# Sums, weight split, stores and turns moved in a streaming encoder layer in float32

## The chip, the cores and the metric

One core of one Trainium2 chip runs the whole step. The metric is the device time of one execution in microseconds (us). Five engines matter: TensorE (PE), whose weight loads (PEld) overlap its multiplications; VectorE (DVE); ScalarE (ACT); GpSimd (POOL); and SyncE (SP), which issues most of the DMAs. ACT issues DMAs as well.

## The reference

A layer works on two inputs: 512 new frames of a prompt, and 64 new frames of a running stream (the sample) with 512 cached frames. The model has 2048 channels.

```python
hn = rmsnorm(x, g_norm1)
proj = hn @ w_in
q, k, v, gb, gc, hc = jnp.split(proj, [...], axis=-1)
q = rmsnorm(q.reshape(B, T, N_HEADS, HEAD_DIM), g_q)      # 8 heads of 128
k = rmsnorm(k.reshape(B, T, N_HEADS, HEAD_DIM), g_k)
...
o_attn = stick_breaking_blocks(q, k_all, v_all, P)        # strictly causal, no softmax
u = gc * hc
o_conv = gb * (conv_w[0] * u[t-2] + conv_w[1] * u[t-1] + conv_w[2] * u[t])
mix = jnp.concatenate([rmsnorm(o_attn, g_attn_out), rmsnorm(o_conv, g_conv_out)], axis=-1)
x = x + mix @ w_out
h2 = rmsnorm(x, g_norm2)
x = x + (jax.nn.silu(h2 @ w_gate) * (h2 @ w_up)) @ w_down  # 5632 hidden channels
```

The outputs are the frames of both inputs, their new keys and values, and the convolution's state.

## The kernel before

The 512 + 64 frames are handled as one block of 576 columns, in two halves of 288. Each operand of a product is split in two rounded parts (hi and lo), and PE multiplies three times: hi with hi, lo with hi, hi with lo. The large products (part of the input projection, the output projection, gate, up and down) are done in blocks by a scheme with seven products instead of eight; the products of a unit are numbered `p_` from 1 to 7, and the units are worked off in a fixed list.

PE's order is the order of the program. Beside it runs a pipeline of generators: `product` and `multiply` call `pipe.tick()` after every step of three multiplications, and a generator that yields n goes on n ticks later. So a number in a `yield` or in `spawn` places a step among PE's multiplications. DVE, ACT, POOL and SP follow the program where `manual_schedule` names them (the start, and everything from the last gate and up units on); elsewhere a scheduler puts their instructions in order by its own estimates.

**The start.** Seven loads bring the prompt's frames (`load_x`), three the sample's (`load_s`), and the first weight comes in quarters (`load_w0`), the first of them on ACT's queue. PE turns frames by multiplying with the identity (`turn_samples`, `turn_x`), ACT copies them out of PSUM, and DVE scales and splits them (lines 374 and 375).

**The first head.** `head(0)` takes up the q product begun at the start and goes on with k and v. `norm_evac` turns a product into 32x32 blocks, squares and sums it; `rest`, `lag` ticks later, lets PE add the sums up over the partitions (L654), forms 1/sqrt (L658 to L663), scales and turns the rows back (L664, L668), scales by channel (L669) and splits (L230, L231). `attend` computes the scores (L723). `third_weight` splits the fourth weight tile (whi, wlo: L177, L178); the third was split in `head(0)`.

**The end.** The down product has 37 units for eight blocks of 256 output channels. `run` adds the products into `acc` tiles (L1592 copies a product out of PSUM, L1612 adds on DVE, L1614 on POOL), and after the last unit of a block `store_y` writes it out. `turn_blocks` turns 32x32 blocks on DVE (L1781) and stores pieces of 32 channels (L1770): four stores for the prompt's frames and four for the sample's. `work`, used for the very last unit, turns on PE (L1789, L1792), copies back on ACT (L1794, L1798) and stores whole rows of 128 channels (L1750, L1752, L1800). Some blocks are "lone" (each half in a tile of its own), others are pairs of halves in one tile. Weights of the down product are loaded into `raw_a` and `raw_b` (L1468), as soon as DVE has used up what was in them.

Of the kernel before, what the change touches and what calls it, by code (L numbers as in the profile page):

```python
# [16 lines left out]
P = 128  # L17
TP = 512
# [76 lines left out]
def tile_hybrid_stream_step(  # L95
# [100 lines left out]
    def third_weight():  # L196
        split_weight(nc.vector)
        yield from ()

    def next_weight():  # L200
        i = pos[0]
        pos[0] += 1
        end = first_out if i < first_out else first_block
        while len(raws) < min(i + 2, end):
            load_weight()
        if i == 2:
            pipe.spawn(third_weight(), 14)
        while len(ready) < min(i + 2, end) and i != 2:
            split_weight(nc.vector)
        while len(raws) < min(i + 3, end):  # L210
            load_weight()
        out = ready[i]
        ready[i] = None
        return out

    pipe = Pipeline()
# [76 lines left out]
    gqs = const.tile([P, 1], F32, name="gqs")  # L293
# [14 lines left out]
    def col(name, i=0):  # L308
        return vec[:, rows[name] + i : rows[name] + i + 1]
# [26 lines left out]
    xin, xsn = {}, {}  # L336
# [6 lines left out]
    def load_s(c):  # L343
        k0, k1 = SCH[c]
        xsn[c] = hpool.tile([TS, (k1 - k0) * P], F32, name=f"xsn{c}")
        nc.sync.dma_start(out=xsn[c], in_=xs[:, k0 * P : k1 * P])

    def turn_samples(c):
        k0, k1 = SCH[c]
# [42 lines left out]
    with tc.manual_schedule(engines={mybir.EngineType.Activation, mybir.EngineType.DVE, mybir.EngineType.SP}):  # L392
# [5 lines left out]
        def load_w0(q):  # L398
            (nc.sync if q else nc.scalar).dma_start(out=raw3[:, 4 * q : 4 * q + 4, :], in_=src[:, 4 * q : 4 * q + 4, :])

        load_w0(0)
        load_x(0)
        load_s(0)
        nc.sync.dma_start(out=g1raw, in_=g_norm1[0].rearrange("(r c) -> r c", c=P))
        load_x(1)
        load_x(2)
# [295 lines left out]
    kw = dict(start=False, skip_group_check=True)  # L702

    def attend(h, st):
        yield 15 + (13 if h == 0 else 0)
        qf, qh, ql, kf, kh, kl, kcT, cV = (st[n] for n in ("qf", "qh", "ql", "kf", "kh", "kl", "kcT", "cV"))

        z = [ps_z.tile([P, 512], F32, tag=f"z{i}", name=f"z{i}") for i in range(3)]
# [45 lines left out]
        kb = st["kb"]  # L754
# [97 lines left out]
    def head(h):  # L852
        st = {}
        st["cK"] = t1.tile([P, TP], F32, tag="cK", name="cK")
        st["cV"] = t1.tile([P, 4, P], F32, tag="cV", name="cV", bufs=2)
        for q in range(4):
            nc.sync.dma_start(out=st["cK"][32 * q : 32 * (q + 1), :].rearrange("t (b c) -> t b c", c=32),
                              in_=ck[:, h, 32 * q : 32 * (q + 1)].rearrange("(b t) c -> t b c", t=32))
        nc.sync.dma_start(out=st["cV"], in_=cv[:, h, :].rearrange("(i p) d -> p i d", p=P))
        for n in ("q", "k"):  # L860
            st[n + "f"] = t1.tile([P, T], F32, tag=n + "f", name=n + "f")
            st[n + "h"] = t1.tile([P, TP], F32R, tag=n + "h", name=n + "h")
            st[n + "l"] = t1.tile([P, TP], F32R, tag=n + "l", name=n + "l")
        st["kb"] = t1.tile([P, T], F32, tag="kb", name="kb")
        q_evac = norm_evac("q", gqs, st["qf"], st["qh"], st["ql"], 13 if h else 25)
        k_evac = norm_evac("k", col("gk"), st["kf"], st["kh"], st["kl"], 16 if h else 6, st["kb"], attend(h, st))
        pipe.spawn(keys_cached(st, 20 if h else 52))
        if h == 0:
            for ps, (a, b) in zip(q0ps, HALVES):
                q_evac(ps, a, b)  # L870
            row_diagonals()
            split_weight(nc.vector)
            pipe.spawn(row_eps(), 23)
            pipe.spawn(row_scale(), 29)
            project(k_evac, (None, "z1"))
        else:
            project(q_evac)
            project(k_evac)
        Ev = t1.tile([P, T], F32, tag="E", name="Ev", bufs=2)

        def v_evac(ps, a, b):
            nc.vector.tensor_tensor(out=Ev[:, a:b], in0=ps, in1=R1[:, a:b], op=ALU.mult)

        project(v_evac, ("z2", None) if h == 0 else (None, None))
        pipe.spawn(values(h, st, Ev))
# [341 lines left out]
    for k_, (n, p_) in enumerate(corder):  # L1227
# [7 lines left out]
        if n == NCU - 1 and p_ in (6, 7, 4):  # L1235
            q = {6: 1, 7: 2, 4: 3}[p_]
# [503 lines left out]
    def store_y(n, c, i):  # L1740
# [22 lines left out]
        def blocks(f, ap):  # L1763

            n = ap.shape[1]
            n_p = max(min(TP - f, n), 0)
            for y, t0, t1, g, eng in ((yp, 0, n_p, f, nc.sync), (ys, n_p, n, f + n_p - TP, nc.scalar)):
                for q in range(4 if t1 > t0 else 0):
                    b0 = cs.start + 32 * q
                    eng.dma_start(out=y[g : g + t1 - t0, b0 : b0 + 32].rearrange("(b t) c -> t b c", t=32),  # L1770
                                  in_=ap[32 * q : 32 * (q + 1), t0:t1].rearrange("t (b c) -> t b c", c=32))

        def turn_blocks():
            if (d, c) in both:
# [8 lines left out]
            blocks(f, all_)  # L1783

        def work():
            yield 4
            po = misc("pot")[:, : 3 * P]
            for q in range(2):
                nc.tensor.transpose(po[:, q * P : (q + 1) * P], src[:, k0 + q * P : k0 + (q + 1) * P], ident)  # L1789
# [12 lines left out]
                put(f0 + k0, ob[:, 0, :])  # L1802
                put(f0 + k0 + P, ob[:, 1, :])
            if rest:
                put(rest[1], obs[:nr], nc.scalar)

        pipe.spawn(work() if n == NU - 1 else turn_blocks())

# [104 lines left out]
```

## Time and profile before

| | |
|---|---|
| median of three runs | 2362.01 us (2360.82 to 2364.43) |
| the profiled execution | 2360.45 us, span 2358.7 us |
| PE busy | 2335.9 us, 99% |
| DVE busy | 1894.6 us, 80% |
| ACT busy | 1134.9 us, 48% |
| POOL busy | 300.3 us, 13% |
| granted clock of PE | 0.999 of full speed |

The profile is of one execution. Its timeline gives for each instruction the start and the duration in us, the engine, the line of the kernel, what is written and read, and in brackets how long the engine was idle before it and what ended that. An engine with a q behind its name (SPq, ACTq) is that engine's sequencer, which issues DMAs. The table of waits adds up such idle times: us in total, times, longest.

### The profile page before, as it was taken

To read this page: it belongs to the slowest core of one execution; us is meant where nothing else is said; L and a number is where in the kernel's file an instruction comes from. 1 tells how busy PE (TensorE), PEld (TensorE's weight loads), DVE (VectorE), ACT (ScalarE), POOL (GpSimd) and SP (SyncE) were. 2 spreads that over 40 slices of the span, in tenths; PEclk is the share of its full clock that TensorE was granted. 3 is DMA by queue.
4 is the path that set the end of the run, shared out by engine and by line. 5 is a ranking of instruction groups with operands and counts; after the bars stand their busy time and mean duration, and the time that the engine had idled before them with its cause. 6 is when DMAs were issued, how large, how long until landed. Compare 5 with 4: busy or idle time off the path is not lost.

```text
span 2358.7 us, 43730 instructions
## 1 busy us (share of the span) xinstructions
PE 2335.9 (99%) x17551; PEld 2325.3 (99%) x17551; DVE 1894.6 (80%) x2828; ACT 1134.9 (48%) x1975; POOL 300.3 (13%) x401
## 2 busy tenths in 40 slices
PE   8999999999999999999999999999999999999998
PEld 8999999999999999999999999999999999999998
DVE  8666666788887899888888888888888777987896
ACT  6655555444445555444444444444444444444443
POOL 1111111422121220000000000000000002431222
PEclk9999999999999999999999999999999999999999
DMA  8565563773468555344344444444444936885554
GB/s 268 153 172 142 139 166 104 240 242 114 124 236 227 173 174 160 122 154 151 122 153 141 134 153 142 133 153 132 144 153 132 359 115 206 223 236 199 190 145 87
DMA packets 588996, 395.75 MB, mean 168 GB/s; under 512 B 100222, under 2 KB 577912, under 8 KB 588792
## 3 DMA queue, kind: packets, MB, share of 16 engines
q1 hardware_dynamic: 574968, 375.95, 51.2%
q0 software_dynamic: 8624, 16.22, 3.3%
q8 instruction: 137, 2.24, 0.4%
q10 hardware_dynamic: 5200, 0.79, 0.2%
q14 instruction: 67, 0.55, 0.1%
HBM read 301.46 MB, written 91.44 MB: 167 GB/s over the span
## 4 chain that ended last, share of the span: by engine, by line
PE 89%; DVE 5%; DMA 3%; issue 1%; ACT 1%; SPq 0%; POOL 0%; ACTq 0%; POOLq 0%; DVEq 0%
PE psy L1582 34%; PE psw L1582 17%; PE pj L221 13%; PE psx L1582 8%; PE psy L1086 6%; PE pjo L221 4%; PE psw L1086 3%; PE psx L1086 1%; DMA raw_a<-in_w_out_dram 1%; DVE whl L231 1%; PE po L794 1%; PE z L723 1%; DVE whl L1058 1%; DMA out_dram<-acc 0%; DVE x L375 0%
## 5 line engine op out<-in xcount | busy, mean ns | idle before, releaser
L1582 PE MATMUL psy<-h_s,whl 128*128 128x288 f32 x2787 | 413.5, 295 | 1.1 <-ACT part L1592 1.1
L221 PE MATMUL pj<-x,whi 128*128 128x288 f32 x1856 | 388.6, 298 | 0.2
L1582 PEld LDWEIGHTS psy<-h_s,whl 128*128 128x128 f32 x2787 | 384.8, 189 | 1.8 <-ACT part L1592 1.8
L231 DVE TENSOR_TENSOR whl<-raw_a,whl 128x1024 fp32r<-128x1024 f32 (+4 forms) x296 | 318.2, 1076 | 54.6 <-ACT whl L230 53.1
L1582 PE MATMUL psw<-t,whl 128*128 128x288 f32 x2400 | 347.0, 294 | 0.0
L1582 PEld LDWEIGHTS psw<-t,whl 128*128 128x128 f32 x2400 | 327.8, 188 | 0.0
L230 ACT CAST whl<-raw_a 128x1024 fp32r<-128x1024 f32 (+4 forms) x296 | 267.5, 906 | 113.1 <-issue 35.4
L221 PEld LDWEIGHTS pj<-x,whi 128*128 128x128 f32 x1856 | 303.6, 189 | 1.4 <-DVE x L375 0.7
L221 PE MATMUL pj<-x,wlo 128*128 128x288 f32 x928 | 274.3, 296 | 0.1
L231 DVE TENSOR_TENSOR whl<-raw_b,whl 128x1024 fp32r<-128x1024 f32 (+5 forms) x190 | 200.2, 1054 | 69.5 <-ACT whl L230 68.2
L230 ACT CAST whl<-raw_b 128x1024 fp32r<-128x1024 f32 (+5 forms) x190 | 164.9, 871 | 170.3 <-issue 73.5
L1592 ACT COPY part<-psy 128x288 f32<-128x288 f32 x242 | 96.4, 398 | 284.9 <-PE psy L1582 262.0
L1582 PE MATMUL psy<-t2t,whl 128*128 128x288 f32 x1212 | 183.0, 294 | 0.8 <-ACT part L1592 0.8
L1582 PE MATMUL psy<-b22m,whl 128*128 128x288 f32 x1212 | 183.3, 295 | 0.1
L221 PEld LDWEIGHTS pj<-x,wlo 128*128 128x128 f32 x928 | 174.7, 188 | 0.7 <-DVE wlo L442 0.3
L1582 PE MATMUL psx<-h_s,whl 128*128 128x288 f32 x1185 | 173.6, 294 | 0.0
L1582 PEld LDWEIGHTS psy<-t2t,whl 128*128 128x128 f32 x1212 | 167.8, 188 | 1.1 <-ACT part L1592 1.1
L1582 PEld LDWEIGHTS psy<-b22m,whl 128*128 128x128 f32 x1212 | 168.2, 188 | 0.4 <-ACT part L1592 0.4
L1582 PEld LDWEIGHTS psx<-h_s,whl 128*128 128x128 f32 x1185 | 162.4, 188 | 0.0
L1361 POOL DMA_DIRECT2D hid_dram<-form x3 | 2.2, 749 | 947.6 <-DVE form L231 947.6
L230 ACT CAST whl<-s 128x1024 fp32r<-128x1024 f32 (+5 forms) x81 | 72.2, 892 | 102.8 <-PE psw L1582 99.4
L1582 PE MATMUL psy<-t,whl 128*128 128x288 f32 x576 | 106.5, 294 | 0.0
(474 smaller groups left out, 4297.4 us busy)
## 6 DMA issues: line engine op xcount, KB each, us to landing
hid_dram<-form SPq DMA_DIRECT2D x147, 288.0 KB, 2.3
raw_a<-in_w_in_dram SPq DMA_DIRECT2D x41, 1024.0 KB, 5.8
raw_a<-in_w_gate_dram SPq DMA_DIRECT2D x22, 1024.0 KB, 5.7
raw_a<-in_w_up_dram SPq DMA_DIRECT2D x22, 1024.0 KB, 5.8
raw_b<-in_w_gate_dram SPq DMA_DIRECT2D x22, 1024.0 KB, 6.5
raw_b<-in_w_up_dram SPq DMA_DIRECT2D x22, 1024.0 KB, 6.6
h_s<-hid_dram SPq DMA_DIRECT2D x10, 2016.0 KB, 12.8
raw_a<-in_w_out_dram SPq DMA_DIRECT2D x16, 1024.0 KB, 6.4
```

Source lines behind the costliest of these rows:

```text
L221: mm(ps, w_[:, k, csl], x_, start=(k == 0 and n == 0), stop=(k == nk - 1 and n == 2))
L230: nc.scalar.copy(out=hi, in_=src)
L231: (lo_eng or nc.vector).tensor_tensor(out=lo, in0=src, in1=hi.bitcast(F32), op=ALU.subtract)
L723: mm(zb[i], a_[:, kk], b_[:, q0:TP], start=(n == 0), stop=False, skip_group_check=True)
L794: mm(po[:, i * P : 512], a_[:, i, :], b_[:, : 512 - i * P], stop=(i == 0 and n == 2), **kw)
L1058: tt(out=whl[:, 1], in0=src, in1=whl[:, 0].bitcast(F32), op=ALU.subtract)
L1086: mm(ps, whl[:, w_, j, :], x_, start=(start and j == 0 and q == 0), stop=(j == m - 1 and q == 2), skip_group_check=True)
L1361: q.dma_start(out=hid_dram[fp][2 * n - 2 : 2 * n].rearrange("f p t -> p f t"), in_=t.bitcast(F32))
L1582: mm(ps, whl[:, w_, j, :], x_, start=(start and j == 0 and q == 0), stop=(j == len(xs_) - 1 and q == 2), skip_group_check=True)
L1592: nc.scalar.copy(out=t, in_=st["y"])
```

## The change

It does four things. In the first head, five numbers of ticks move. At the start, the sample's first frames are loaded by ACT's queue ahead of the first weight quarter, which then follows the prompt's first frames in the program. At the end, SP issues the sample's stores that ACT issued in `turn_blocks`. And `work`, with its turns on PE, is used for the last units of three blocks instead of one; for the two added ones it begins after nine ticks and gives its rest to SP.

```diff
-            pipe.spawn(third_weight(), 14)
+            pipe.spawn(third_weight(), 19)
...
-        nc.sync.dma_start(out=xsn[c], in_=xs[:, k0 * P : k1 * P])
+        (nc.sync if c else nc.scalar).dma_start(out=xsn[c], in_=xs[:, k0 * P : k1 * P])
...
-        load_w0(0)
         load_x(0)
         load_s(0)
+        load_w0(0)
...
-        yield 15 + (13 if h == 0 else 0)
+        yield 15 + (4 if h == 0 else 0)
...
-        q_evac = norm_evac("q", gqs, st["qf"], st["qh"], st["ql"], 13 if h else 25)
-        k_evac = norm_evac("k", col("gk"), st["kf"], st["kh"], st["kl"], 16 if h else 6, st["kb"], attend(h, st))
+        q_evac = norm_evac("q", gqs, st["qf"], st["qh"], st["ql"], 13 if h else 31)
+        k_evac = norm_evac("k", col("gk"), st["kf"], st["kh"], st["kl"], 16 if h else 15, st["kb"], attend(h, st))
...
-            for y, t0, t1, g, eng in ((yp, 0, n_p, f, nc.sync), (ys, n_p, n, f + n_p - TP, nc.scalar)):
+            for y, t0, t1, g in ((yp, 0, n_p, f), (ys, n_p, n, f + n_p - TP)):
                 for q in range(4 if t1 > t0 else 0):
...
-                    eng.dma_start(out=y[g : g + t1 - t0, b0 : b0 + 32].rearrange("(b t) c -> t b c", t=32),
+                    nc.sync.dma_start(out=y[g : g + t1 - t0, b0 : b0 + 32].rearrange("(b t) c -> t b c", t=32),
...
         def work():
-            yield 4
+            quick = n == NU - 1
+            yield 4 if quick else 9
...
-                put(rest[1], obs[:nr], nc.scalar)
-
-        pipe.spawn(work() if n == NU - 1 else turn_blocks())
+                put(rest[1], obs[:nr], nc.scalar if quick else nc.sync)
+
+        pipe.spawn(work() if n in sorted(last)[-3:] else turn_blocks())
```

DVE in the first head, before, from the end of the q chain to the end of the k chain (ql is the split of q, wlo the low part of the fourth weight, sums, ms, t, r, Ek and kf the steps of k):

```order
L231 TENSOR_TENSOR ql<-qf,qh 128x512
L178 TENSOR_TENSOR wlo_812<-raw_a,whi_811 128x1024
L678 TENSOR_REDUCE sums<-sq 128x9
L178 TENSOR_TENSOR wlo_812<-raw_a,whi_811 128x1024
L658 TENSOR_SCALAR ms<-ss,rpad_t 128x18
L850 STREAM_TRANSPOSE kcT<-cK 128x512
L661 TENSOR_SCALAR t<-y 128x18
L662 TENSOR_TENSOR t<-t,ms 128x18
L663 TENSOR_SCALAR r<-t,y 128x18
L664 TENSOR_TENSOR Ek<-Ek,r 128x576
L668 STREAM_TRANSPOSE kf<-Ek 128x576
```

The same place after the change (the first ms, t, t and r are now those of q):

```order
L658 TENSOR_SCALAR ms<-ss,rpad_t 128x18
L178 TENSOR_TENSOR wlo_829<-raw_a,whi_828 128x1024
L661 TENSOR_SCALAR t<-y 128x18
L678 TENSOR_REDUCE sums<-sq 128x9
L662 TENSOR_TENSOR t<-t,ms 128x18
L178 TENSOR_TENSOR wlo_829<-raw_a,whi_828 128x1024
L663 TENSOR_SCALAR r<-t,y 128x18
L664 TENSOR_TENSOR Eq<-Eq,r 128x576
L668 STREAM_TRANSPOSE qf<-Eq 128x576
L850 STREAM_TRANSPOSE kcT<-cK 128x512
L658 TENSOR_SCALAR ms<-ss,rpad_t 128x18
L231 TENSOR_TENSOR ql<-qf,qh 128x512
```

The fourth weight moved from behind the q chain to inside it, ahead of the q rows' scaling and turning, and the k chain from behind the weight to behind both.

SP at the end, before, around the blocks of acc_t2z and acc_m1z (one pair) and the next (raw_a and raw_b are the down weights):

```order
L1468 DMA raw_b<-in_w_down_dram 128x10x256
L1770 DMA out_dram<-acc_t2z 32x16x32 x4
L1770 DMA out_dram<-acc_m1z 32x16x32 x4
L1468 DMA raw_a<-in_w_down_dram 128x10x256
L1770 DMA out_dram<-acc_z 32x16x32 x4
L1770 DMA out_dram<-acc_ax 32x16x32 x4
```

The same place after the change:

```order
L1468 DMA raw_b<-in_w_down_dram 128x10x256
L1770 DMA out_dram<-acc_t2z 32x16x32 x4
L1770 DMA out_dram<-acc_t2z 32x2x32 x4
L1770 DMA out_dram<-acc_m1z 32x16x32 x4
L1770 DMA out_dram<-acc_m1z 32x2x32 x4
L1468 DMA raw_a<-in_w_down_dram 128x10x256
L1770 DMA out_dram<-acc_z 32x16x32 x4
L1770 DMA out_dram<-acc_z 32x2x32 x4
```

The four small stores of each block, which stood on ACT, now stand on SP behind the four large ones, and the weight load behind all sixteen.

PE in the first of the two units that turn on PE now, in the product that follows the unit's second (before, only multiplications stand here; the line numbers of `work` are one higher after the change):

```order
L1582 MATMUL psw<-h_s_9012,whl 128x288 x3
L1582 MATMUL psw<-b22m_10290,whl 128x288 x3
L1790 MATMUL pot<-ident,acc_21412 128x128 x2
L1793 MATMUL pot<-ident,acc_21412 32x128
L1582 MATMUL psw<-t_6_10169,whl 128x288 x3
L1582 MATMUL psw<-h_s_9011,whl 128x288 x3
```

Two full turns and one of the last 32 frames stand among the multiplications of a running product.

More of the change, by code (lines that the diff above doesn't have):

```diff
@@ L1766, in blocks @@
             n_p = max(min(TP - f, n), 0)
-            for y, t0, t1, g, eng in ((yp, 0, n_p, f, nc.sync), (ys, n_p, n, f + n_p - TP, nc.scalar)):
+            for y, t0, t1, g in ((yp, 0, n_p, f), (ys, n_p, n, f + n_p - TP)):
                 for q in range(4 if t1 > t0 else 0):
                     b0 = cs.start + 32 * q
-                    eng.dma_start(out=y[g : g + t1 - t0, b0 : b0 + 32].rearrange("(b t) c -> t b c", t=32),
-                                  in_=ap[32 * q : 32 * (q + 1), t0:t1].rearrange("t (b c) -> t b c", c=32))
+                    nc.sync.dma_start(out=y[g : g + t1 - t0, b0 : b0 + 32].rearrange("(b t) c -> t b c", t=32),
+                                      in_=ap[32 * q : 32 * (q + 1), t0:t1].rearrange("t (b c) -> t b c", c=32))
         def turn_blocks():
```

## Prediction

> **What bounds the kernel now.** I read the page first, then the table of waits for PE, then the timeline of each engine where a wait stands, and the chain of work that ended last.
>
> ```profile
> span 2358.7 us, 43730 instructions
> PE 2335.9 (99%) x17551; PEld 2325.3 (99%) x17551; DVE 1894.6 (80%) x2828; ACT 1134.9 (48%) x1975; POOL 300.3 (13%) x401
> ```
>
> PE is without work for 2358.7 - 2335.9 = 22.8 us. The change takes away no multiplication, so 22.8 us is all that it could win. Where PE waits, the table of waits says (us in total, times, longest):
>
> ```profile
> PE psx_s L352 <- DMA xsn<-in_x_sample_dram: 5.4, 1, 5.4
> PE ss L654 <- DVE sums L678: 2.5, 2, 1.7
> PE psy L1582 <- ACT part L1592: 1.9, 3, 0.8
> PE psw L1582 <- DVE acc L1612: 0.6, 1, 0.6
> PE pot L1789 <- POOL acc L1614: 0.2, 1, 0.2
> ```
>
> These five are the waits that the edits can reach: the start, the sums of the first head, and the last 50 us. Together they are 10.6 us. From 100 us to 2240 us the edits leave PE's order as it is, and I cost that stretch at nothing: DVE and ACT swap a few steps in the second and third head, where PE waits for neither.
>
> **The start.** The sample's first frames now go out on ACT's queue, ahead of the first weight quarter, instead of behind the prompt's frames on SP's.
>
> ```profile
> 1.32 3.94 DMA xsn<-in_x_sample_dram
> 5.40 0.66 PE psx_s L352 x4
> 8.09 0.53 DVE x L374
> 26.68 0.83 DVE x L375
> ```
>
> This is the chain: the load, the turns on PE, then DVE making frames back to back until 27.5 us, so what PE wins at 5.4 us reaches DVE and the rest. But PE's turn also waits for the identity and its neighbours on POOL:
>
> ```profile
> 2.39 2.45 POOL L268 TENSOR_SCALAR_AFFINE_SELECT acA<-acA 128x128 f32<-128x128 f32 x7
> ```
>
> POOL ends at 4.84. So the turn moves from 5.40 to 4.9 at best, 0.5 us. The load is issued at about 0.84 instead of 1.32, which is 0.5 us too. The first weight quarter leaves 0.5 us later; its cast stands behind two copies on ACT, at 7.9 us, and I see no wait there now. If that cover were gone, the start would lose up to 0.5 us. I take 0.35 us won, between -0.5 and +0.5, nearer the gain because the bytes on the way are the same and only their order changes.
>
> **The first head.** Five numbers move: the sums of q are multiplied (L654) at tick 31 instead of 25, those of k at 15 instead of 6, the fourth weight is split at 19 instead of 14, and attention begins 4 + 15 ticks after the sums of k instead of 13 + 15. 15 + 19 = 34 = 6 + 28, so PE meets the scores (L723) after the same multiplications as now.
>
> ```profile
> 43.11 0.40 PE L654 MATMUL ss<-sums,acA 128*128 128x18 f32 x2 [0.80 <-DVE sums L678]
> 51.96 0.37 PE L654 MATMUL ss<-sums,acA 128*128 128x18 f32 x2 [1.72 <-DVE sums L678]
> 63.39 0.28 PE L723 MATMUL z<-qh,kh 128*128 128x256 f32 x1
> 49.13 1.05 ACT L177 CAST whi<-raw_a 128x1024 fp32r<-128x1024 f32 x1 [0.40 <-DMA raw_a<-in_w_in_dram]
> 50.22 1.23 DVE L178 TENSOR_TENSOR wlo<-raw_a,whi 128x1024 fp32r<-128x1024 f32 x1 [0.76 <-ACT whi L177]
> 51.36 0.45 DVE L678 TENSOR_REDUCE sums<-sq 128x9 f32<-128x288 f32 x1
> 52.86 0.17 DVE L658 SCALAR_TENSOR_TENSOR ms<-ss,rpad_t 128x18 f32<-128x18 f32 x1
> ```
>
> The two waits are 0.80 and 1.72 us, 2.52 in all. The sums of q are ready at 43.1, and PE got to them at 42.3 and will now come six ticks later (a tick is three multiplications, 0.40 us) with the diagonals (1.3 us) in between, at about 46: that wait goes. Those of k hang on the fourth weight: ACT stands at the weight's load until 49.13, and DVE does a half of the weight (50.22) ahead of the sums (51.36). The new order on DVE keeps that half ahead of the sums. They end at about 52.0. PE got there at 51.96 - 1.72 = 50.24; 0.80 earlier and nine ticks later is 53.0. That wait goes too, with 1 us to spare.
>
> What is late next are the scores. In the new order both halves of the fourth weight stand ahead of the rest of the q chain, and the k chain comes behind that. The durations:
>
> ```profile
> 46.49 0.78 DVE L668 STREAM_TRANSPOSE qf<-Eq 128x576 f32<-128x576 f32 x1
> 48.12 0.62 ACT L230 CAST qh<-qf 128x512 fp32r<-128x512 f32 x1
> 55.81 0.78 ACT L669 ACTIVATE kf<-kf,vec 128x576 f32<-128x576 f32 x1 [2.28 <-DVE kf L668]
> 57.16 0.56 DVE L231 TENSOR_TENSOR kl<-kf,kh 128x384 fp32r<-128x384 f32 x1 [0.65 <-ACT kh L230]
> ```
>
> From 50.22: two halves, the sums and the small steps between, 3.0 us, to 53.2; the q rows scaled and turned, 0.15 + 0.8 + 0.78, to 54.9; on ACT the scaling (0.78, as for k) and qh (0.62), a little overlapped, to 56.3; the k chain's two ACT steps 0.5, to 56.8; its small DVE steps and one half of the values between them 1.1, to 57.9; scaled and turned 1.55, to 59.45; scaled on ACT and cast 1.35, to 60.8; kl 0.55, to 61.35. PE, 2.52 us earlier, arrives at 63.39 - 2.52 = 60.87. So about 0.5 us comes back as a wait at L723, and 2.0 us are left. The load of the weight bounds this from both sides: landing as early as PE gains at the start, 2.5 us are left; 2 us later, none. The cached keys and weight of the second head are issued some 2 us later, since DVE's turn of the first head's cached keys is; they have 10 us before ACT asks for them.
>
> **The end.** Now the sample's stores are issued by ACT, and ACT stands at them:
>
> ```profile
> 2313.80 4.71 ACTq L1770 DMA_DIRECT2D out_dram<-acc  x8
> 2318.55 0.40 ACT L1592 COPY part<-psy 128x288 f32<-128x288 f32 x1 [4.47 <-DMA out_dram<-acc]
> 2342.84 2.01 ACTq L1770 DMA_DIRECT2D out_dram<-acc  x4
> 2319.01 0.67 PE L1582 MATMUL psy<-t2t,whl 128*128 128x288 f32 x3 [0.82 <-ACT part L1592]
> 2345.40 0.67 PE L1582 MATMUL psy<-h_s,whl 128*128 128x288 f32 x3 [0.79 <-ACT part L1592]
> 2347.87 0.67 PE L1582 MATMUL psw<-h_s,whl 128*128 128x288 f32 x3 [0.58 <-DVE acc L1612]
> ```
>
> A copy that frees PE's bank (L1592) waits behind eight stores for 4.47 us, and PE waits 0.82 us for the copy; the same again at 2345 (0.79), and DVE, held by the late cast behind it, costs 0.58. With the stores on SP, ACT has none of these, and the POOL wait of 0.2 hangs on the same late copies: 2.19 + 0.2 = 2.4 us go. DVE also loses six turns there.
>
> Against this stand TensorE's turns for two more units: four lone blocks of three turns, and a pair of pairs with 2 + 2 + 3 + 3, 22 in all. The chain of work prices three:
>
> ```profile
> 2352.44 0.22 PE pot L1789 x2
> 2352.66 0.12 PE pot L1792
> ```
>
> 22 x 0.113 = 2.5 us, all on PE. The turned rows are added at least nine ticks (3.6 us) before PE asks; the adds of now end within 2 to 3 us, so I charge no wait.
>
> [...]
>
> SP now issues 16 stores for a finished pair where it issued 8, and the next weight load of the down product stands behind them.
>
> ```profile
> 2271.43 1.96 SPq L1770 DMA_DIRECT2D out_dram<-acc_t2z  x4
> 2257.55 5.21 SPq L1770 DMA_DIRECT2D out_dram<-acc_z  x8
> 2264.49 0.40 SPq L1468 DMA_DIRECT2D raw_b<-in_w_down_dram  x1
> 2271.92 0.73 ACT L230 CAST whl<-raw_b 128x640 fp32r<-128x640 f32 x1 [2.10 <-DMA raw_b<-in_w_down_dram]
> 2272.68 0.82 DVE L231 TENSOR_TENSOR whl<-raw_b,whl 128x640 fp32r<-128x640 f32 x1 [0.97 <-ACT whl L230]
> 2274.95 5.94 PE psy L1582 x45
> ```
>
> Four stores take 1.96 us, 0.49 each. Sixteen from 2257.55 end at 2265.4, so the load slips from 2264.49 by 1 us. ACT already waits 2.10 us for it, and DVE ends that operand at 2273.5. PE's 45 multiplications from 2274.95 are three products; the second, at 2274.95 + 1.98 = 2276.93, is the first to use it. The slack is 3.4 us, so a slip of 1 us is hidden four times over. The copies behind that cast on ACT are not late, since the 1.95 us of stores there are gone.
>
> Last, the tail behind PE's last work. SP's last stores wait for ACT's (waits of SP in the last 13 us):
>
> ```profile
> SPq L1752 <- DMA out_dram<-raw_b: 1.5, 2, 1.0
> SPq L1750 <- DMA out_dram<-raw_b: 0.4, 1, 0.4
> ```
>
> With the slow 32-row stores gone from the last 15 us and another order of the semaphores, I expect part of these 1.9 us back, 0.6 (between 0 and 1).
>
> The end: -2.4 + 2.5 - 0.6 = -0.5 us. It would be +2.5 if no wait went, -1.5 if all of them and the whole tail did.
>
> **The sum.** -0.35 - 2.0 - 0.5 = -2.85 us. The profiled execution took 2360.45 (1.75 outside its span), so 2357.6 for one like it. The median of the runs is 2362.01, 1.56 above it; against that I predict 2359.2. That is 0.12%; about 0.2% (4.7 us) is what a measurement of this kernel tells from no change.
>
> **The rivals.** (1) *The loads fall behind the stores on SP: slower.* If an issue in a row of 16 costs more than 0.65 us, the load slips by over 3.4 us and PE waits. The eight issues at 2257.55 took 5.21 us, a gap included, 0.65 each. At 0.8 us the load leaves at 2270.35, 5.9 us late, PE waits 2.4 us for it, at four such loads: 9.6 us, 2368.8. Against it: 0.49 for four in a row, with ACT issuing at the same time.
>
> (2) *The scores take the place of the sums.* If the fourth weight lands 2 us later, or DVE's new order runs worse than I added up, PE waits 2.5 us at L723 in place of 2.5 at L654: 2361.2. For it: my sum already has 0.5 us of it.
>
> (3) *A turn costs PE its whole record.*
>
> ```profile
> L1789 PE MATMUL pot<-ident,acc 128*128 128x128 f32 x8 | 1.7, 290 | 0.6 <-DVE acc L1612 0.3 <-POOL acc L1614 0.2
> ```
>
> At 290 ns, 22 turns are 6.4 us instead of 2.5: 2363.1. Against it: the chain has two in 0.22 us, since they are pipelined. [...]
>
> (4) *More goes than I count.* All of the start (0.5), all of the sums (2.5), the whole tail and DVE's relief (1.5 to 2): about -4.8, 2357.2, at the edge of what can be told.
>
> **How the numbers follow.** Forecast 0.64; rival 1 0.08; rival 2 0.13; rival 3 0.05; rival 4 0.10. Only rival 1 is slower by over 0.2%: 0.08. Rival 4 and a little of the forecast are faster by over 0.2%: 0.12. Within: 0.80. The range runs from rival 4 less 1.4 us of scatter (the three runs spread 3.6 us) to rival 3: 2355.8 to 2363.1; rival 1 is left out.
>
> **What would show it.** Right: no wait of PE at L654 in the first head, a wait of under 1 us at L723 near 61 us; the first turn near 4.9 us; no wait of PE for L1592 after 2240 us; 22 more turns 0.11 us apart; down loads issued about 1 us later relative to the stores, with no wait of PE. Wrong: a wait of PE for whl after 2260 us (rival 1), 2 us at L723 (rival 2), turns spaced 0.27 us (rival 3).

## The result, and the profile after

The changed kernel takes 2357.62 us (median of 18 runs, 2355.32 to 2360.17), the kernel before 2361.86 (18 runs on the same chip, 2359.14 to 2364.43): a ratio of 0.9983, 95% interval 0.9977 to 0.9989. That is 4.0 us less. The gain is less than the 0.2% that the prediction took for the least that a measurement tells, but a ratio of 1 lies outside the interval. The forecast was 2359.2, the range 2355.8 to 2363.1. The profiled execution took 2357.63 us, 2.82 less than that of before; the sum had said 2.85. Of all runs below, one of the kernel with the sample's stores on SP alone took 3250.84 us at a granted clock of 0.655, and its ratio leaves that run out.

The head of the page after, and four rows of PE's table of waits (us in total, times, longest):

```profile
span 2355.9 us, 43774 instructions
PE 2335.7 (99%) x17573; PEld 2326.5 (99%) x17573; DVE 1890.2 (80%) x2822; ACT 1138.5 (48%) x1989; POOL 298.6 (13%) x401
```

```profile
PE psx_s L352 <- POOL acA L268: 4.9, 1, 4.9
PE psy L1086 <- DVE whl L1058: 2.8, 3, 1.0
PE ss L500 <- ACT sq L230: 1.7, 1, 1.7
PE z L723 <- DVE kl L231: 0.2, 1, 0.2
```

The rows for L654 are gone, and the first turn waits 0.5 us less, as forecast. The second row was 1.8 us before: a wait has grown in the middle, where I had charged nothing.

**The first head** went as worked out. PE's timeline after, then DVE's:

```profile
45.74 0.29 PE L654 MATMUL ss<-sums,acA 128*128 128x18 f32 x2
52.34 0.29 PE L654 MATMUL ss<-sums,acA 128*128 128x18 f32 x2
60.78 0.39 PE L723 MATMUL z<-qh,kl 128*128 128x256 f32 x1 [0.21 <-DVE kl L231]
```

```profile
50.87 0.44 DVE L678 TENSOR_REDUCE sums<-sq 128x9 f32<-128x288 f32 x1
60.16 0.56 DVE L231 TENSOR_TENSOR kl<-kf,kh 128x384 fp32r<-128x384 f32 x1 [1.39 <-ACT kh L230]
```

Both sums are met without a wait, those of k 1.0 us after they are ready. kl ends at 60.7; the forecast was 61.35, and the cast of the fourth weight started 0.58 us earlier than before (48.55 for 49.13). PE waits 0.21 us for kl (forecast 0.5). By the starts of the first three scores the wait costs 0.57 us: they are at 63.39, 63.51 and 63.63 before, at 60.19, 60.78 and 61.00 after. So at the third score PE leads by 2.63 us, of which 0.5 to 0.8 is the start's.

**The middle** gives most of that lead back. First before, then after: ACT's cast for a form of the attention (hf, one of the blocks and differences of blocks that the seven products take), and PE's products in the convolution (L1086).

```profile
476.38 0.43 ACT L230 CAST hf<-o_ob 128x288 fp32r<-128x288 f32 x1 [3.75 <-DMA form_dram<-hf]
489.46 3.41 PE L1086 MATMUL psx<-x,whl 128*128 128x288 f32 x24 [1.45 <-DVE cv L1110]
```

```profile
475.34 0.43 ACT L230 CAST hf<-o_ob 128x288 fp32r<-128x288 f32 x1 [4.99 <-DMA form_dram<-hf]
482.38 0.40 PE L1086 MATMUL psy<-x,whl 128*128 128x288 f32 x1 [0.47 <-ACT whl L1055]
483.64 3.31 PE L1086 MATMUL psy<-x,whl 128*128 128x288 f32 x23 [0.86 <-DVE whl L1058]
488.43 3.44 PE L1086 MATMUL psx<-x,whl 128*128 128x288 f32 x24 [1.48 <-DVE cv L1110]
...
733.86 5.03 PE L1086 MATMUL psy<-forms,whl 128*128 128x288 f32 x36 [0.56 <-ACT part L1095]
745.94 5.06 PE L1086 MATMUL psy<-forms,whl 128*128 128x288 f32 x36 [0.70 <-ACT part L1095]
```

ACT wants a buffer whose store has not landed. It stood 3.75 us for it before and 4.99 after (and 0.31 at a store just ahead), so of the 2.6 us by which ACT came earlier 1.0 is left, and the casts behind it make PE wait twice. PE leaves the place 1.03 us ahead. At 734 and 746 us ACT stands at weights still on their way (3.13 and 3.28 us; 2.81 and 2.82 before), PE waits 0.56 and 0.70 us (0.23 and 0.25 before), and at 751 us its lead is 0.09. This second loss need not be a price of the lead: between 660 and 752 us PE loses 0.2 to 1.1 us against the profile of before in each of the other profiles, the end alone, which lags, 0.5.

**A stretch at half clock.** The windows of before, then of after, behind the sums of the second norm (columns: window, its length, busy time of the five engines with instructions, granted clock, DMA share, GB/s):

```profile
884.00:886.00 2.00, 2.00 (x11) 2.00 (x12) 2.00 (x4) 0.89 (x2) 0.00 (x0) 0.67 0.99 321
886.00:888.00 2.00, 2.00 (x10) 2.00 (x9) 2.00 (x3) 1.05 (x1) 0.00 (x0) 0.50 1.09 392
888.00:890.00 2.00, 2.00 (x16) 2.00 (x16) 2.00 (x4) 0.93 (x1) 0.00 (x0) 0.97 0.75 271
```

```profile
884.00:886.00 2.00, 1.86 (x14) 1.86 (x15) 2.00 (x5) 0.89 (x2) 0.00 (x0) 1.00 0.94 293
886.00:888.00 2.00, 2.00 (x18) 2.00 (x17) 2.00 (x3) 0.87 (x1) 0.00 (x0) 1.00 1.08 390
```

PE's own rows, before and after:

```profile
884.16 4.47 PE L1582 MATMUL psy<-h_s,whl 128*128 128x288 f32 x21
```

```profile
884.38 2.96 PE L1582 MATMUL psy<-h_s,whl 128*128 128x288 f32 x21
```

At 882 to 884 us PE does little but wait for these sums. Before, the three windows lack 0.66 + 1.00 + 0.06 = 1.72 us of full clock, which is half the clock for 3.4 us, and the same 21 multiplications took 4.47 us instead of 2.96. After, the gap is no shorter (PE idle 1.70 us for the first sum, 1.37 before) and the clock stayed. The changed kernel goes into this place 0.22 us behind the kernel before and comes out 1.33 ahead. The change does not touch this stretch.

**The end.** No wait for L1592 is left behind 2240 us. PE's last turn starts at 2350.90 us (2353.32 before), 5.0 us ahead of the span's end (5.4 before).

### The profile page after: what moved, and what is told of

Same layout as the page of the kernel before. It is cut to its first block, busy times and chain, and to the rows that moved or that the text cites. A ratio compares the mean times of both kernels' runs of the same rounds, so it can differ in the third digit from the quotient of the medians.

```text
span 2355.9 us, 43774 instructions
## 1 busy us (share of the span) xinstructions
PE 2335.7 (99%) x17573; PEld 2326.5 (99%) x17573; DVE 1890.2 (80%) x2822; ACT 1138.5 (48%) x1989; POOL 298.6 (13%) x401
## 4 chain that ended last, share of the span: by engine, by line
PE 86%; DVE 8%; DMA 3%; ACT 2%; issue 1%; POOL 0%; SPq 0%; DVEq 0%; ACTq 0%; POOLq 0%
PE psy L1582 34%; PE psw L1582 17%; PE pj L221 13%; PE psx L1582 9%; PE psy L1086 5%; PE psw L1086 3%; PE psx L1086 1%; DMA raw_a<-in_w_out_dram 1%; DVE wlo L178 1%; DMA raw_a<-in_w_in_dram 1%; DVE whl L231 1%; DVE whl L1058 1%; PE z L723 1%; PE pjo L221 1%; PE po L794 1%
## 5 line engine op out<-in xcount | busy, mean ns | idle before, releaser
L1592 ACT COPY part<-psy 128x288 f32<-128x288 f32 x242 | 96.5, 399 | 273.9 <-PE psy L1582 271.2
```

The costliest lines, as they stand in the source:

```text
L1592: nc.scalar.copy(out=t, in_=st["y"])
```

## The experiments

Each kernel was timed against the kernel before on the same chip, except two that ran once (split stores, and POOL's constant later). PE's times in the profiles repeat closely: from its first psx near 2310 us to its last turn it took 40.80 to 40.89 us in five that have the end of the changed kernel (changed, raw_c later, the end alone, POOL's constant later, the second norm's sums later), and 42.44 to 42.86 in three with the end of before (before, the start alone, the first head alone). So single steps are read from profiles and whole times from ratios.

**The start alone.**

```diff
-        nc.sync.dma_start(out=xsn[c], in_=xs[:, k0 * P : k1 * P])
+        (nc.sync if c else nc.scalar).dma_start(out=xsn[c], in_=xs[:, k0 * P : k1 * P])
...
-        load_w0(0)
         load_x(0)
         load_s(0)
+        load_w0(0)
```

> The kernel before with the edit of the start alone (the sample's first frames issued first on ACT's queue, the first weight quarter behind them). Theory (the load, the turn and DVE's frames are one chain): PE's first turn at 4.9 us instead of 5.40, DVE's first frame at 7.6 instead of 8.09, PE at the first scores (L723) at about 62.9 instead of 63.39, and at most 0.5 us off the end, a ratio of 0.9998. Rival (the later weight quarter takes it back): the first frames are earlier, the scores still at 63.4, and the time is unchanged.

Measured 2360.87 us, ratio 1.0003 (0.9994 to 1.0012). Its timeline:

```profile
2.38 2.45 POOL L268 TENSOR_SCALAR_AFFINE_SELECT acA<-acA 128x128 f32<-128x128 f32 x7
4.63 0.66 PE L352 MATMUL psx_s<-ident,xsn 64*128 64x64 f32 x4 [4.63 <-DMA xsn<-in_x_sample_dram]
```

PE turned at 4.63 us while POOL was still at acA, until 4.83. POOL ends there at 4.83 or 4.84 us, whether the first turn starts at 4.58 us (two units' turns back on DVE), at 4.90 (changed) or at 5.40 (before). So POOL does not hold the turn, though the table of the changed kernel names it; the load does, 3.7 to 4.5 us from its issue in the profiles with this edit. DVE's first frame came 0.77 us earlier (7.32), the third score 0.80 (62.83), so up to there nothing is taken back and the rival's price isn't seen. At 752 us 0.43 us of it is left. In the time it is lost in the scatter: the prompt's frames, which PE needs next, made it wait between 0 and 2.2 us in the same place of the other profiles.

**The first head alone.**

```diff
-            pipe.spawn(third_weight(), 14)
+            pipe.spawn(third_weight(), 19)
...
-        yield 15 + (13 if h == 0 else 0)
+        yield 15 + (4 if h == 0 else 0)
...
-..., 13 if h else 25)
+..., 13 if h else 31)
-..., 16 if h else 6, st["kb"], attend(h, st))
+..., 16 if h else 15, st["kb"], attend(h, st))
```

> The kernel before with the five numbers of the first head alone. Theory: no wait of PE at L654, the first scores (L723) between 60.9 and 61.4 us instead of 63.39, a wait there of under 0.5 us, and so 2.0 to 2.5 us won at 65 us. What becomes of it is the question. If it is carried to the end, the time falls by 2.0 to 2.5 us (0.9990). If the stores of the attention forms hold ACT at 475 us, as the trace of the changed kernel has it (PE's product at L1086 came 2.6 us earlier into that place and 1.0 us earlier out of it), PE waits 1 to 1.5 us more for whl at 480 to 485 us and the time falls by about 1 us (0.9996). Rival on record (the scores take the place of the sums): a wait of about 2.5 us at L723 and no gain.

Measured 2358.95 us, 0.9992 (0.9983 to 1.0001). Neither L654 nor L723 is in its table of waits. In its profile the prompt's frames came 2.2 us late, so it could not tell what becomes of a large lead. All the profiles together can: where PE stands against the kernel before at the third product of the scores (about 63 us) and at the first full psw of the convolution (L1086, about 493 us), in us, a minus for earlier.

| kernel | at 63 us | at 493 us |
|---|---|---|
| end alone (below) | +1.62 | +1.53 |
| turns alone (below) | +0.35 | +0.28 |
| first head alone | -0.25 | -0.35 |
| start alone | -0.80 | -0.90 |
| changed, two units' turns back on DVE | -1.15 | -1.25 |
| the changed kernel | -2.63 | -1.03 |
| changed, raw_c later (below) | -2.34 | -3.50 |

A lead of up to 1.2 us, or a lag, goes through nearly unchanged; the lead of 2.6 comes out as 1.0, and leads of 2.2 to 2.6 us in four more profiles with the same program there as 0.9 to 1.6. The fifth and the sixth kernel have the same program up to 2240 us: PE came 1.5 us later in one and left the place no later.

**raw_c later.** One weight load moves behind three more stores of the forms.

```diff
             for f, src in ((1, b11), (2, b21), (3, b22)):
                 put(f, src, nc.vector)
                 yield 2
+            if k == 2:
+                bt["raw"] = apool.tile([P, 2048], F32, tag="oa", name="raw_c")
...
+                call_columns([2])
...
-            if k == 1:
-                bt["raw"] = apool.tile([P, 2048], F32, tag="oa", name="raw_c")
...
-                call_columns([2])
```

> The changed kernel with one megabyte of weight (raw_c, L1021) loaded three stores later among the stores of the attention forms, so that three stores of 288 KB go ahead of it on SP's queue. Theory (the first head's gain is lost at 475 us, where ACT waits 4.99 us for a store of the forms to land): ACT gets its buffer back about 2.5 us earlier, PE's waits for whl at 482 and 484 us (0.47 and 0.86) go, and the product that starts at 488.4 us (L1086, psx) starts at 486.9 to 487.2 as PE's lead of 2.6 us over the kernel before comes through. At the end 1 to 1.5 us less than the changed kernel if nothing later takes it; nothing if the weights from w_out at 733 to 746 us take it again, for which ACT already waits 3.1 to 3.3 us. Rival (the whole stretch is bound by the bytes on the way, not by their order): the wait moves from the store to the weight, PE still starts at 488.4.

Measured 2356.05 us, 0.9978 (0.9970 to 0.9987). SP after the change, then SP, ACT and PE with raw_c later:

```profile
465.60 0.50 SPq L1021 DMA_DIRECT2D raw_c<-in_w_in_dram  x1
466.19 12.83 SPq L580 DMA_DIRECT2D form_dram<-hf  x11
```

```profile
461.70 5.76 SPq L580 DMA_DIRECT2D form_dram<-hf  x5
467.51 0.72 SPq L1021 DMA_DIRECT2D raw_c<-in_w_in_dram  x1
...
470.66 0.97 ACT L230 CAST hf<-o_ob 128x288 fp32r<-128x288 f32 x2 [0.43 <-DMA form_dram<-hf]
...
485.96 3.44 PE L1086 MATMUL psx<-x,whl 128*128 128x288 f32 x24 [0.60 <-DVE cv L1110]
```

ACT's wait of 4.99 us is 0.43, the two waits of PE are gone, and psx starts at 485.96 instead of 488.43 (486.9 to 487.2 was expected). So the place was set by the order on the queue, not by the bytes: the rival falls. PE leaves it 3.50 us ahead, 1.16 more than it came with, since waits that the kernel before has there are shorter too (psx 0.60 instead of 1.45). It keeps 2.94 us at 765 us; at the sums of the second norm (L500) it then waits 3.1 us, and 1.28 are left. In the timings the gain over the changed kernel is small, and the two intervals overlap.

**The sample's stores on SP alone.**

```diff
-            for y, t0, t1, g, eng in ((yp, 0, n_p, f, nc.sync), (ys, n_p, n, f + n_p - TP, nc.scalar)):
+            for y, t0, t1, g, eng in ((yp, 0, n_p, f, nc.sync), (ys, n_p, n, f + n_p - TP, nc.sync)):
```

> The kernel before with the sample's stores of the down units issued by SP instead of ACT, nothing else. Theory: no wait of PE for part (L1592) and for acc (L1612) behind 2240 us, which were 2.2 us, the tail 0 to 1 us shorter: 2 to 3 us off the time (0.999). Sixteen stores in a row at 0.5 to 0.6 us each make the weight loads of the down product 1 to 2 us later, within their slack of 3.4 us. Rival (the loads fall behind the stores): PE waits for whl behind 2260 us, up to 2.4 us at each of four loads, and the kernel is up to 9.6 us slower.

Measured 2365.89 us, 1.0017 (1.0008 to 1.0026): slower. PE gained what the theory says and more, and it waited for no weight longer than before. But SP's queue ran on without it (SP's issues, then a row of SP's waits):

```profile
2315.89 38.00 SPq L1770 DMA_DIRECT2D out_dram<-acc  x48
...
2354.48 4.04 SPq L1770 DMA_DIRECT2D out_dram<-acc  x8
...
2361.45 0.43 SPq L1752 DMA_DIRECT2D out_dram<-acc  x1
```

```profile
SPq L1770 <- DMA out_dram<-raw_b: 13.7, 2, 11.9
```

PE's last turn starts at 2349.89 us, the span ends at 2364.2, 14.3 us later. The first row isn't 38 us of issuing: SP stands still in it for 13.7 us, 11.9 of them up to 2344.87, until, as the waits have it, a store that ACT issued at 2343.41 (out_dram<-raw_b, rows of the last unit) has landed. Only then do the last 23 of the 32-row stores go out, 16 of them after 2349.99, one behind another at about 0.5 us each. DVE had turned their blocks by 2334.06, 2343.05 and 2344.58. Without that wait, by an estimate from these times, they would be out by 2351 instead of 2358.5. By that most of the long tail is SP's wait for ACT's store and not the number of stores; no run takes the two apart.

**The changed kernel with two units' turns back on DVE.**

```diff
-        pipe.spawn(work() if n in sorted(last)[-3:] else turn_blocks())
+        pipe.spawn(work() if n in sorted(last)[-1:] else turn_blocks())
```

> The changed kernel with only the last unit turned by TensorE, the two units ahead of it by DVE again (22 turns of TensorE less, and their stores as 32-row blocks by SP). If a turn costs PE 0.113 us, its spacing in the chain: 2.5 us less of PE's work, and the time is 2.5 us less than that of the changed kernel unless DVE's turns bring waits or a longer tail. If a turn costs PE its record of 0.29 us: 6.4 us less. If the turns by TensorE were what took the waits of the last 40 us away (DVE held up by its turns): PE waits again for acc (L1612) or for the bank of pot, 2 us or more together, and the time is that of the changed kernel or longer.

Measured 2363.11 us, 1.0011 (1.0002 to 1.0020): slower than before, and by the ratios 6.6 us slower than the changed kernel. PE has none of its waits back and 2.6 us less of work, but the tail is 9.3 us longer: 14.35 us, again SP's queue, with the same wait for ACT's stores in it (13.4 us). In the changed kernel's waits there is no such row.

**The end alone, and the turns alone** (the sample's stores left on ACT).

```diff
-            yield 4
+            yield 4 if n == NU - 1 else 9
-        pipe.spawn(work() if n == NU - 1 else turn_blocks())
+        pipe.spawn(work() if n in sorted(last)[-3:] else turn_blocks())
```

The end alone has the edit of the stores too, and gives the rest of the two added units to SP.

> The kernel before with the two edits of the end alone: the sample's stores by SP and the last three units turned by TensorE. By the traces of the parts: PE's waits at the end are worth 4.1 us, not the 2.4 that the table of waits gives, since each costs about 0.3 us more than its row; 22 turns cost 2.6; the tail is 0.4 shorter: 1.9 us less than before, 0.9992. By the sum on record: 0.5 us less, 0.9998.

> The kernel before with the last three units turned by TensorE, and the sample's stores left on ACT. Theory: SP has no 32-row stores of these units any more, and ACT none after 2320 us, so the waits at 2345 to 2350 us go (3.0 us of the 4.1) and the one at 2319 us stays (1.1): 2.6 us of turns - 3.0 - 0.4 of tail = 0.8 us less than before (0.9997). If the move to SP is what frees PE, and not the turns, the gain is not there and the time is 2 us longer than before.

Measured 2360.32 us, 0.9996 (0.9988 to 1.0005), and 2359.28 us, 0.9994 (0.9985 to 1.0003). The ratios cannot tell these forecasts apart; the profiles can.

**Each turn twice.** The 34 turns of `work` are made twice over the same place.

```diff
-            for q in range(2):
+            for q in (0, 0, 1, 1):
...
                 nc.tensor.transpose(po[:nr, 2 * P :], rest[0], ident)
+                nc.tensor.transpose(po[:nr, 2 * P :], rest[0], ident)
```

> The changed kernel with each of the 34 turns by TensorE of the last three units made twice in a row, the second over the first (34 turns more, no other work). If a turn costs PE its spacing: 22 turns made the difference of 2.6 us between the changed kernel and the one without them (PE from 2268 us to its end 82.36 against 79.77 us), 0.118 us each, so 34 cost 4.0 us and the ratio to the kernel before is near 1.0000. [...]

Measured 2359.64 us, 0.9993 (0.9984 to 1.0002).

These five experiments are read from one pair of rows per kernel, PE's first psx of a late unit and its last turn. Before, stores on SP alone, changed, and each turn twice:

```profile
2310.88 0.56 PE L1582 MATMUL psx<-t2t,whl 128*128 128x288 f32 x3
2353.32 0.27 PE L1792 MATMUL pot<-ident,acc 128*32 128x128 f32 x1
```

```profile
2311.65 0.57 PE L1582 MATMUL psx<-t2t,whl 128*128 128x288 f32 x3
2349.89 0.27 PE L1792 MATMUL pot<-ident,acc 128*32 128x128 f32 x1
```

```profile
2310.06 0.56 PE L1582 MATMUL psx<-t2t,whl 128*128 128x288 f32 x3
2350.90 0.27 PE L1793 MATMUL pot<-ident,acc 128*32 128x128 f32 x1
```

```profile
2310.99 0.55 PE L1582 MATMUL psx<-t2t,whl 128*128 128x288 f32 x3
2355.18 0.27 PE L1794 MATMUL pot<-ident,acc 128*32 128x128 f32 x1
```

| kernel | first psx to last turn | last turn to the span's end | sum |
|---|---|---|---|
| before | 42.44 | 5.4 | 47.8 |
| stores on SP alone | 38.24 | 14.3 | 52.5 |
| turns alone | 41.61 | 4.6 | 46.2 |
| end alone | 40.83 | 5.1 | 45.9 |
| changed | 40.84 | 5.0 | 45.8 |
| changed, two units' turns back on DVE | 38.25 | 14.4 | 52.6 |
| changed, each turn twice | 44.19 | 5.0 | 49.2 |

The waits were worth 42.44 - 38.24 = 4.2 us. The 22 turns cost 40.84 - 38.25 = 2.6 us, 0.118 each, and 34 more cost 3.35 (4.0 was expected), 0.099 each. By the sums the end alone is 1.9 us shorter than before, as its first forecast has it, and the turns alone 1.6 (0.8 was expected). The first of these prices is the difference of two kernels, and has in it whatever else the turns change there. The stores on SP are worth 0.3 us once the turns are there, and cost 4.7 without them.

**Split stores.** Every 32-row store of the down units in two of 16 rows.

```diff
-                    nc.sync.dma_start(out=y[g : g + t1 - t0, b0 : b0 + 32].rearrange("(b t) c -> t b c", t=32),
...
+                    to = y[g : g + t1 - t0, b0 : b0 + 32].rearrange("(b t) c -> t b c", t=32)
+                    fr = ap[32 * q : 32 * (q + 1), t0:t1].rearrange("t (b c) -> t b c", c=32)
+                    for r0 in (0, 16):
+                        nc.sync.dma_start(out=to[r0 : r0 + 16], in_=fr[r0 : r0 + 16])
```

> The changed kernel with every 32-row store of the down units split in two of 16 rows, so that a finished pair has 32 stores in a row on SP where it has 16; the bytes are the same. Rival 1 on record (the weight loads fall behind the stores): 16 more issues at 0.5 to 0.6 us put the next load 8 to 10 us later than in the changed kernel, past its slack of 3.4 us, and PE waits for whl 4 to 6 us at each of the last loads behind 2260 us; 10 us or more in all. If the second half of a split store costs much less than the first, or the slack is larger than worked out, PE waits for less than 2 us in all.

One run: 2375.58 us, 13.1 above the median of before. SP and a row of PE's waits:

```profile
2255.61 16.58 SPq L1773 DMA_DIRECT2D out_dram<-acc_z  x32
2272.29 0.40 SPq L1468 DMA_DIRECT2D raw_b<-in_w_down_dram  x1
```

```profile
PE psy L1582 <- ACT part L1592: 14.1, 4, 6.5
```

These 32 issues take 0.52 us each, where the changed kernel's 16 of twice the rows take 0.50 (2256.72 to 2264.69), so the load comes 7.5 us later than the changed kernel's (2264.78), and PE waits 13.9 us at three places behind 2260 us. PE's row names part, because the copy stands on ACT behind the cast that waits for the weight (in the changed kernel the cast starts at 2271.86 us, after 2.87 us at the load, and the copy at 2272.49). Rival 1 is a true mechanism. In the changed kernel the loads from 2264 us on were issued 0.3 to 1.9 us later than before (1.1 to 2.7 against PE, which is 0.8 ahead), within their slack.

**POOL's constant later.**

```diff
+            if kt == 2:
+                make_same()
```

`make_same` holds the steps that set up the last part of acA, the seven of L268 among them.

> The changed kernel with POOL's last constant (acA, L268, seven steps that end at 4.83 us) made later, behind the first turns. If POOL releases the first turn, as the profile names it, the turn starts earlier than 4.87 us, when the sample's frames have landed. If the load releases it (issued at 0.85 us; in the kernel before the same load took 4.08 us from its issue to the turn), the turn still starts at 4.9 us, and POOL's end at 4.83 was a coincidence.

In its one run the seven steps stand where they had been (2.38 to 4.83 us), so this edit tells nothing. The question is answered by the start alone, above.

**The second norm's sums later.** The finding at 884 us asked for the change's own trick at another place. (One of the two sums also goes to the bank z2, so that it doesn't hold up the next product.)

```diff
             multiply(x, n, 2, True)
-            if n == 0:
-                row_scale2()
-            add(0, 0, x, st["p1"])
-            done(0, 0, x, st["p1"])
+            def close():
+                yield 7
+                row_scale2()
+                done(0, 0, x, st["p1"])
+            if n == 0:
+                pipe.spawn(close())
+            else:
+                add(0, 0, x, st["p1"])
+                done(0, 0, x, st["p1"])
```

> The changed kernel with the two sums of the second norm (ss, L500, which PE meets at 881 us and waits for, 1.70 us in its table of waits) multiplied one product later, behind the next 24 multiplications, and one of them in a PSUM bank that is free there; the arithmetic is the same. Theory: PE has no gap at 882 to 884 us, since the sums are ready at 883.6 us and PE gets to them at 884.6; the gap cost 2.1 us (1.85 idle and the overlap lost around it), and with it goes the chance of a stretch at half clock behind it, which cost 1.55 us in 6 of the 10 profiles so far. If the product behind finds its operand ready: 2 us less than the changed kernel and up to 1 us more for the clock, 2354.5 to 2355.5 where the kernel before takes 2361.5 (0.9970 to 0.9975). Rival (DVE is the bound there, which makes the next operands back to back): PE waits for whl at 885 to 892 us in place of the sums, the half clock may still come, and the time is that of the changed kernel (0.9983).

Measured 2356.67 us, 0.9975 (0.9964 to 0.9985). The wait for the sums is gone and the clock stays at 1.00, but PE waits 2.4 us at 888 to 904 us (whl, part, gs), and at 910 us it stands where the changed kernel's profile does. So the rival is right about that profile. That a typical run wins the half clock is argued: the interval overlaps that of the changed kernel (0.9977 to 0.9989).

**Both together**, raw_c later and the sums of the second norm later:

> The changed kernel with both of the edits tried apart: raw_c loaded three stores later, and the two sums of the second norm multiplied one product later. Theory: the first brings PE to 765 us 2.9 us ahead of the kernel before (it was 0.1 us ahead in the changed kernel), of which 1.7 us went at the sums of the second norm; with those later it keeps at least what it had behind them, 1.3 to 1.5 us more than the changed kernel, and no stretch at half clock follows at 884 us. Together 1.5 to 2.5 us less than the changed kernel, a ratio to the kernel before of 0.9970 to 0.9976. Rival (DVE's operands at 885 to 900 us set the pace whatever comes ahead): PE waits there for whl and for part by as much as it came earlier, and the ratio stays at 0.9978, that of the first edit alone, or above.

Measured 2355.05 us, 0.9970 (0.9958 to 0.9982), the lowest of all ratios, though its interval overlaps those of both edits alone. Its windows:

```profile
882.00:884.00 2.00, 2.00 (x18) 2.00 (x17) 1.94 (x2) 0.00 (x0) 0.00 (x0) 1.00 0.88 286
884.00:886.00 2.00, 2.00 (x17) 2.00 (x17) 1.97 (x3) 1.46 (x2) 0.00 (x0) 1.00 1.09 394
```

PE has no gap there. Its six runs lie between 2354.80 and 2355.46 us, where 18 runs of the changed kernel spread over 4.9 us; why they scatter less isn't shown. The rival's waits are there too (1.2 us for part, 0.6 for gs). At 912 us PE is 2.46 us ahead of the kernel before, and 1.32 with raw_c alone, whose profile has the half clock. The 1.14 us between them are less than the 1.55 of the half clock, so here too no more than that is seen to be won.

## Why the prediction was right, and where it was not

The time lies in the range, 1.6 us under the forecast, and within 0.2% of before. The sum for the profile, -2.85 us against -2.82, was right by errors that cancel, and that is luck. Of the 2.35 us that the start and the first head were to give, 0.09 is left at 751 us; the end gave 2.0 us instead of 0.5; a stretch at half clock, which was in no sum, gave 1.55; and 0.8 us went in other places.

- **The start, -0.35.** The turn and DVE's first frame moved 0.5 us (7.58 instead of 8.09). The bound "POOL ends at 4.84, so the turn moves to 4.9 at best" was wrong: POOL does not hold it. Alone the edit shows no gain in the time.
- **The first head, -2.0.** Right up to the scores, step by step, and rival 2 did not come. The step that failed is the sentence that from 100 to 2240 us the edits leave PE's order as it is and cost nothing. PE's order is the same, but the place at 475 us lets through only about a microsecond of lead. At 740 us, where every other profile stands worse than that of before, the rest goes in this one. I had looked for waits that the edits move, and not for waits that an earlier PE would meet.
- **The end, -0.5.** It is -2.0. The turns were priced right (2.6 for 2.5) and the tail too (-0.4 for -0.6). Its bound of -1.5 was a slip as well (2.5 - 2.4 - 1.9 is -1.8), and the result lies beyond both. The mis-sized term is the waits: 4.2 us instead of 2.4, because I took the table's idle times for the loss. Set against the same multiplications with the stores on SP alone, the four waits (0.82, 0.79, 0.58 and 0.21 us) cost 1.1, 1.1, 0.9 and 0.4. Two places where PE was idle 0.12 and 0.06 us, and which I did not count, cost 0.4 each. The rows of before around the second wait show why:

```profile
2344.05 0.56 PE L1582 MATMUL psw<-h_s,whl 128*128 128x288 f32 x3
...
2345.91 0.58 PE L1582 MATMUL psy<-b22m,whl 128*128 128x288 f32 x3
```

Groups of three start 0.40 us apart, so the one behind 2344.05 was due at 2344.45. It started at 2345.40, and the next at 2345.91, 0.51 later: 1.06 us lost, where the table gives 0.79. A record overlaps its neighbours, and the idle time is counted from where the last one ends.

- **What the turns are for.** I charged them as a pure cost. They are what makes the move to SP pay: with rows of 128 channels a unit has two to five stores instead of eight or sixteen, and without them SP's queue ends 9 us later, most of it, by the estimate above, in a wait for a store of ACT's. Rival 1 had the right resource and the wrong place: not the weights (in the changed kernel no wait of PE for whl behind 2260 us), but the tail of the kernels without the turns.
- **Rival 3**, the whole record of 290 ns per turn, falls: 0.10 to 0.12 us each. The traces have 0.27 us as the length of a record (L1792 before, L1793 after), but not as the price: at 0.27 us the 34 turns more would have cost 9.2 us, and they cost 3.35.
- **Rival 4** named 2357.2 us, close to what came, but not for its reasons: the sums' 2.5 us were won and lost again.
- **The half clock**, 1.55 us between the two profiles, was in no sum. It came in 7 of the 12 profiles that have the gap, and with the same program it came and did not (below), so it is no gain of the change, and the two profiles taken by themselves would leave 1.3 us for the change.

What the two profiles leave open is the size of the gain: the medians are 4.2 us apart, the two profiles without the half clock 1.3. The other profiles answer most of it. Four of them have the program of before up to 2240 us (before, the end alone, the turns alone, stores on SP alone), and six that of the changed kernel up to 880 us (changed, two units' turns back on DVE, each turn twice, split stores, POOL's constant later, the second norm's sums later). On average PE is 2.6 us earlier in the six at 470 us, and 1.3 us at 752. With the 2.0 us of the end that makes 3.3, inside the 2.6 to 5.4 us of the interval, and the half clock came about as often in both (in 2 of the 4, and in 3 of the 5 that have the gap). It is an estimate, since within each group PE's place differs by 0.9 to 2.0 us at 752 us. By it the start and the first head are worth 1.3 us and not 2.35, and the profile of before was one in which the frames came early. The ratios of the three parts alone add up to 2.1 us of gain, with too wide an interval to say whether the parts help each other.

## What to carry to other kernels

Ask of every microsecond won early which later place will let it through: here a store that ACT already waited for (3.75 us before) was a ceiling, before PE waited at it at all. Price a wait of a pipelined PE by the starts of the groups around it, not by the idle time in the table (1.06 us against 0.79 above). Read a long row of issues for the waits in it. And judge edits of a queue and of the stores on it together: here the move of the stores alone is 4 us slower, and with the turns it is 1.9 us less by the profiles.

## What the hardware showed

- A stretch at half clock followed the gap near 882 to 886 us in 7 of the 12 profiles that have the gap, and in neither of the two without it. In the profile of before it is half the clock for 3.4 us, and against that of the changed kernel it cost 1.55 us. Kernels with the same program up to there fell on both sides (before: yes; the end alone and the turns alone: no). A gap of 2.2 us with two multiplications in it was followed by it in one execution (before) and not in another (the first head alone), and one of 3.0 us (the turns alone) was not. What sets it off is not shown.
- A 32-row store cost its queue 0.49 to 0.59 us to issue where one follows another (before: four on SP in 1.96 us, eight of the sample's on ACT in 4.71), and one of 16 rows as much (0.50 us for 32 rows and 0.52 for 16 in the rows at 2256 us). There the number of stores counts and not their bytes.
- A queue can also stand for the other's: 11.9 us of SP's, with the stores on SP alone, went by until one store of ACT's had landed.
